# Second layer's shift and scale summed elementwise on VectorE, ScalarE and GpSimd beside the last merges and the output projection of the first

## The chip, the cores and the metric

The kernel runs as one program on one core of a Trainium2 chip. The metric is device time in microseconds (us), from launch to the last store, the median over runs. TensorE (PE in the rows) multiplies matrices, with a row of its own for its weight loads (PEld); VectorE is DVE, ScalarE ACT, GpSimd POOL; SyncE (SP) issues most of the loads. Each engine works through its own instructions strictly in order.

## The reference

Two layers of a backbone with four parallel token mixers (A windowed attention, B RWKV-7, C attention, D gated DeltaNet), model width 2048, 256 context and 256 latent tokens, all fp32. What matters here is the modulation and the tail of a layer:

```
shift, scale, gate = split(silu(c) @ w_mod + b_mod, 3)          # per layer, for latent tokens
sh_c, sc_c, gt_c   = split(silu(c_ctx) @ w_mod + b_mod, 3)      # the same for context tokens
h  = rms(x) * (1 + scale) + shift                               # input of the layer
x  = x + gate * (sum_i sigmoid(pm @ g_up[i] + g_b[i]) * (y_i @ w_br[i])) @ w_out
```

`w_mod` of one layer is 2048 x 6144. There are only two vectors to multiply it with, `c` and `c_ctx`, so the product is 2 x 6144 numbers for 50 MB of weights.

## The kernel before

**Tiles.** Activations stand feature-first: 16 tiles of 128 features by 512 tokens. Most products are made of float32r matmuls with operands split in a high and a low part: `weights` (L370) loads a weight tile of 128x512 into `wr` on SyncE's queue, ScalarE casts it to `wh`, VectorE subtracts to get `wl`, and `mm3` issues three matmuls for each 128x128 block. `wh` and `wl` have 4 buffers each, `wr` has 5.

**The modulation.** `w_mod` is cut in 12 chunks of 512 columns (0 to 3 shift, 4 to 7 scale, 8 to 11 gate), each of 16 tiles of 128 rows by 512 columns, 256 KB. `mod_unit` (L477) handles 4 such tiles: 4 loads on SyncE's queue, then 4 matmuls with 32 columns of `s32` (the two silu vectors, in columns 6 and 7, zeros around them) as weights and the tile as the moving operand, each into its own 32 rows of one PSUM bank. 16 units sum 4 chunks in one bank; after the last a copy to `ms`, four small matmuls with `sel` (which bring the numbers back to feature-first) and additions of the bias give four chunks of `mod`.

**The stage of the change.** In `layer`, the first layer ends with `drain`, which pumps what is left in the queue of generators: the steps of `merge_gen` for the branches C and D (in a step, 18 matmuls give one output tile of gate and branch, with a tanh on ScalarE and a multiply and an add on VectorE). Then `out_proj` makes 16 output tiles `x`, each of 4 weight tiles and 48 matmuls, and behind each of them it calls two units of `next_mods`: 32 units, chunks 0 to 7 of the second layer's modulation, in banks of the pool `mx`. The remaining 16 units (the first layer's generator goes on with the gate chunks 8 to 11 of the second layer) follow in `run`, 8 ahead of `build_h` and 8 among the first projections of layer 1. The loads of all these go to `mr`, which has 16 buffers.

**What sets the order.** The code states work in a sequence, and a scheduler that fills each engine's list by its own planning costs decides the order in which the instructions stand on each engine. That order is fixed when the program is built: an engine whose next instruction waits does not pass over it.

Of the kernel before, what the change touches and what calls it, by code (L numbers as in the profile page):

```python
# [12 lines left out]
AF = mybir.ActivationFunctionType  # L13
ALU = mybir.AluOpType
# [39 lines left out]
_PO, _o = {}, 0  # L54
# [116 lines left out]


MXB = 3
NL2 = 3
MODS = (2, 3)
MODL = (((0, 8, 12),), ())
# [11 lines left out]
class Kern:  # L188
# [8 lines left out]
    def nm(s, t):  # L197
# [2 lines left out]

    BUFS = {t: 2 for t in ("ar AT01 AT10 AT11 tok0 tok1 wc bo vt dl nb dec Dk ktok vs pT pt aq "
                           "iR sw po it").split()}
    BUFS.update(mr=16, Z=3, U=3, S=3, vs=3, dZ=3, Sd=4, Rb=16, po=3, ms=1, wr=5, wh=4, wl=4, QD=3, qg=3, dl=4, vn=2,
                nb=4, dec=4)

    BX = ({}, dict(vtok=2, cz=2))
# [234 lines left out]

    def next_mods(s, pool):

        for n in (0, 4, 8):
            for u in range(16):
                s.mod_unit(s.l + 1 if n < 8 else s.l, tuple(range(n, n + 4)), u, [(pool, "mr")], True, s.bank if n < 8 else None)
                yield

    def mod_gen(s, u):
        s.mod_unit(*u, [(s.wp, "wr")])  # L450
# [26 lines left out]
    def mod_unit(s, l, chunks, u, pools, acc=False, bank=None):  # L477


        nc = s.nc  # L480
        i, nch = u // 4, len(chunks)
        first, last = u == 0, u == 4 * nch - 1
        raws = []
        for g in range(4):
            pool, tag = pools[g % len(pools)]
            raw = s.tl(pool, [128, 512], tag)
            nc.sync.dma_start(raw, s.i["wmod"][l, chunks[i], u % 4 * 4 + g])
            raws.append(raw)
        if first or not acc:
            s.mps = (bank or s.big)()  # L490
        ps = s.mps
        for g in range(4):
            s.mm(ps[32 * g:32 * g + 32, :], s.s32[:, u % 4 * 4 + g, 6 - 2 * i:38 - 2 * i], raws[g],
                 not acc or first, not acc or last)
        if last if acc else first:
            s.ms = s.tl(s.rp, [128, 512], "ms")
            nc.scalar.copy(s.ms, ps)
        elif not acc:
            s.tt(s.ms, s.ms, ps, ALU.add)
        if last:  # L500
            par, mod = s.lp[l]
            bo = _PO["bm"][0]
            w = 2 * nch
            p2 = (bank or s.big)()
            for f in range(4):
                s.mm(p2[:, w * f:w * f + w], s.ms[:, f * 128:(f + 1) * 128], s.c("sel", 0, w))
            pv = p2[:, 0:4 * w].rearrange("p (f i c) -> p i f c", f=4, c=2)
            for i, n in enumerate(chunks):
                s.tt(mod[:, n * 4:n * 4 + 4, :], pv[:, i], wide(par[:, bo + n * 4:bo + n * 4 + 4], 2), ALU.add)


    def sumsq(s, acc, x, first):
# [876 lines left out]
    def out_proj(s, xs_pool):  # L1389
        nc, l, acc = s.nc, s.l, s.acc  # L1390
        t0 = 0 if l == 0 else CTX
        n = T - t0
        ah, al = [], []
        for dt in range(KT):
            hi = s.tl(s.R, [128, T], "Rb", F32R)[:, 0:n]
            lo = s.tl(s.R, [128, T], "Ra", F32R)[:, 0:n]
            s.act(hi, acc[dt], AF.Copy, 0.5)
            s.stt(lo, acc[dt], 0.5, hi.bitcast(F32), ALU.mult, ALU.subtract)
            ah.append(hi)
            al.append(lo)  # L1400
        sqa = s.tl(xs_pool, [128, T], "sqa")[:, 0:n]
        xn = []
        if l == 0:
            s.modn = s.next_mods(xs_pool)
        for dt in range(KT):
            xo = s.tl(s.rp, [128, T], "po")[:, 0:n]
            nc.sync.dma_start(xo, s.i["xT"][dt] if l == 0 else s.x1[dt])
            ps = s.big()[:, 0:n]
            for qt in range(4):
                w = s.weights(s.i["wout"][l, dt, qt], [128, 4, 128])  # L1410
                for k in range(4):
                    kk = qt * 4 + k
                    s.mm3(ps, (w[0][:, k, :], w[1][:, k, :]), (ah[kk], al[kk]), kk == 0, kk == 15)
            x = xs_pool.tile([128, n], F32, tag=f"x{dt}", name=s.nm("x"))
            for hf in range(n // 256):
                sl = slice(hf * 256, hf * 256 + 256)
# [54 lines left out]
    def layer(s):  # L1471
# [8 lines left out]
        with s.tc.tile_pool(name=f"mix{l}", bufs=1) as pool:  # L1480
# [10 lines left out]
        s.rho = 0.0  # L1491

    def run(s):
        tc, nc = s.tc, s.nc
        with ExitStack() as ctx:
# [56 lines left out]
            for l in range(L):  # L1552
# [2 lines left out]
                s.par, s.mod = s.lp[l]  # L1555
                s.layer()
                with tc.tile_pool(name=f"xs{l}", bufs=1) as xp:
                    xn, sqa = s.out_proj(xp)
                    rsb = s.rms_rows(sqa, xp)
                    if l + 1 < L:  # L1560
                        s.l = l + 1
                        s.par, s.mod = s.lp[l + 1]
                        for _ in range(8):
                            next(s.modn)
                        s.build_h(xn, rsb)
# [35 lines left out]
```

## Time and profile before

| | us |
|---|---|
| median of 3 runs (2844.48 to 2854.17) | 2846.87 |
| the profiled execution's own time | 2842.45 |
| its span in the trace | 2840.7 |
| PE busy | 2710.4 (95% of the span) |
| DVE busy | 1856.9 (65%) |
| ACT busy | 1260.0 (44%) |
| POOL busy | 180.0 (6%) |

Busy time is a sum of instruction durations with overlaps counted once. Two neighbouring instructions of VectorE or ScalarE overlap by some 0.08 us in their records, so that the distance from start to start is what one costs in a row of many. A matmul's record is longer than the distance to the next one for the same reason.

### The profile page before, as it was taken

The page shows a single profiled execution, that of the slowest core. Times are in us where ns is not written, and L with a number is a line of the kernel's source. Part 1 is how long each engine was busy: PE and PEld are TensorE (multiplying, and loading weights), DVE is VectorE, ACT ScalarE, POOL GpSimd, SP SyncE. Part 2 cuts the span into 40 slices and gives each one's busy share as a digit, 9 for nine tenths or more (in the row PEclk, how much of TensorE's full clock was granted, in tenths as well). Part 3 has the DMA queues.
Part 4 walks back from the last instruction along what each step waited for, and adds up shares of the span by engine and source line. Part 5 has one row for each costly group of instructions (what it writes and reads, how often), then busy time and mean ns, then how long its engine had stood idle before and what let it go on. Part 6 is the DMA issues. An engine that isn't in the chain of part 4 may idle for free. (4 is left out here: it accounts for less than half of the span.)

```text
span 2840.7 us, 52626 instructions
## 1 busy us (share of the span) xinstructions
PE 2710.4 (95%) x19438; PEld 2056.8 (72%) x19438; DVE 1856.9 (65%) x5255; ACT 1260.0 (44%) x2705; POOL 180.0 (6%) x436
## 2 busy tenths in 40 slices
PE   7998999999999998999999999999999999999897
PEld 3676666677787786777787756776777887867897
DVE  4337776656676777876553354777765687678775
ACT  3334333333354555655442244444443356455553
POOL 0000000000010101000000000010010001100000
PEclk9999999999999999999999999999999999999999
DMA  9753243322342323224537886322332442433465
GB/s 346 261 189 127 83 131 105 127 83 68 115 121 88 100 72 115 79 82 134 170 114 248 279 282 203 96 78 78 93 91 75 157 143 88 133 98 88 144 190 159
DMA packets 210049, 385.80 MB, mean 136 GB/s; under 512 B 24640, under 2 KB 37824, under 8 KB 209792
## 3 DMA queue, kind: packets, MB, share of 16 engines
q1 hardware_dynamic: 199872, 351.23, 39.6%
q0 software_dynamic: 9920, 31.20, 2.9%
q8 instruction: 153, 2.51, 0.4%
q14 instruction: 104, 0.85, 0.1%
HBM read 346.95 MB, written 35.39 MB: 135 GB/s over the span
## 5 line engine op out<-in xcount | busy, mean ns | idle before, releaser
L283 PE MATMUL big<-Rb,wh 128*128 128x512 f32 (+1 forms) x3280 | 1100.7, 364 | 21.3 <-ACT Rb L1325 10.0
L283 PE MATMUL big<-Ra,wh 128*128 128x512 f32 (+1 forms) x2128 | 777.3, 365 | 8.9 <-DVE po L315 5.6
L375 ACT CAST wh<-wr 128x512 fp32r<-128x512 f32 x712 | 438.8, 619 | 762.8 <-PE big L283 576.2
L283 PEld LDWEIGHTS big<-Rb,wh 128*128 128x128 f32 x3280 | 612.1, 191 | 128.8 <-ACT Rb L1325 14.0
L312 DVE TENSOR_TENSOR wl<-wr,wh 128x512 fp32r<-128x512 f32 x712 | 488.4, 688 | 304.3 <-ACT wh L375 280.3
L283 PE MATMUL big<-Ra,wl 128*128 128x512 f32 (+1 forms) x1616 | 597.2, 370 | 6.3 <-DVE wl L312 6.3
L283 PEld LDWEIGHTS big<-Ra,wh 128*128 128x128 f32 x2128 | 407.5, 192 | 84.3 <-issue 9.5
L283 PE MATMUL big<-Rb,wl 128*128 128x512 f32 (+1 forms) x1088 | 380.4, 350 | 1.1 <-DVE wl L312 1.1
L283 PEld LDWEIGHTS big<-Ra,wl 128*128 128x128 f32 x1616 | 310.3, 192 | 53.4 <-DVE wl L312 8.6
L283 PEld LDWEIGHTS big<-Rb,wl 128*128 128x128 f32 x1088 | 207.6, 191 | 26.2 <-DVE wl L312 1.5
L312 DVE TENSOR_TENSOR iX<-iX,it 128x60 f32<-128x60 f32 (+24 forms) x744 | 181.4, 244 | 15.7
L312 DVE TENSOR_TENSOR it<-iB,iX 128x60 f32<-128x60 f32 (+24 forms) x744 | 172.7, 232 | 15.6
L315 DVE SCALAR_TENSOR_TENSOR po<-po,big 128x512 f32<-128x512 f32 (+1 forms) x128 | 70.6, 552 | 77.1 <-PE big L283 74.2
L283 PE MATMUL big<-Rb,wr 128*128 128x256 f32 (+1 forms) x448 | 111.3, 417 | 5.0 <-ACT po L309 3.1
L309 ACT ACTIVATE sw<-S,wc 128x64 f32<-128x64 f32 x96 | 33.4, 348 | 176.2 <-DVE S L315 153.5
L283 PE MATMUL big<-mr,s 128*32 128x512 f32 x384 | 85.2, 617 | 18.3 <-DMA mr<-in_wmod 18.3
L309 ACT ACTIVATE po<-big,gb 128x512 f32<-128x512 f32 (+1 forms) x128 | 74.2, 579 | 57.3 <-PE big L283 41.2
L283 PEld LDWEIGHTS big<-Rb,wr 128*128 128x128 f32 (+1 forms) x448 | 70.6, 179 | 24.1 <-issue 7.3
L283 PE MATMUL sc<-vt,AT 64*64 64x64 f32 x512 | 71.3, 238 | 0.0
L315 DVE SCALAR_TENSOR_TENSOR cz<-raw,par,cz 128x508 f32<-128x508 f32 (+3 forms) x96 | 67.2, 700 | 5.4 <-ACT cz L309 5.0
L632 DVE TENSOR_REDUCE mx<-mx 128x1 f32<-128x512 f32 (+1 forms) x96 | 57.1, 599 | 18.7 <-PE mx L283 17.5
L283 PE MATMUL sc<-vt,tok 64*64 64x64 f32 x448 | 67.5, 232 | 0.0
(371 smaller groups left out, 4033.0 us busy)
## 6 DMA issues: line engine op xcount, KB each, us to landing
wr<-in_win SPq DMA_DIRECT2D x440, 256.0 KB, 2.7
mr<-in_wmod SPq DMA_DIRECT2D x320, 256.0 KB, 5.0
wr<-in_wbr SPq DMA_DIRECT2D x128, 256.0 KB, 2.7
wr<-in_wout SPq DMA_DIRECT2D x128, 256.0 KB, 3.1
wr<-in_wmod SPq DMA_DIRECT2D x64, 256.0 KB, 3.9
wr<-in_gup SPq DMA_DIRECT2D x64, 256.0 KB, 2.6
x<-in_xT SPq DMA_DIRECT2D x16, 256.0 KB, 5.4
po<-y SPq DMA_DIRECT2D x16, 256.0 KB, 3.0
```

The lines of the kernel that those rows point to most:

```text
L283: s.nc.tensor.matmul(o, l, r, start=start, stop=stop)
L309: s.nc.scalar.activation(o, i, f, bias=bias, scale=scale, **k)
L312: s.nc.vector.tensor_tensor(o, a, b, op)
L315: s.nc.vector.scalar_tensor_tensor(o, a, sc, b, op0, op1)
L375: s.nc.scalar.copy(hi, raw)
L632: nc.vector.tensor_reduce(mx[:, hc], ps[:, 0:nk], AX.X, ALU.max)
```

## The change

The second layer's shift and scale (chunks 0 to 7) are no longer made of matmuls over 128 tiles. A tile `mr` is multiplied by the two scalars of its 128 rows, once for `c` and once for `c_ctx`, and summed over the 16 tiles of a chunk: for `c` in `ma0` by one VectorE instruction a tile (multiply by the scalar, add the sum so far); for `c_ctx` by ScalarE into `mt` (two buffers) and an addition into `ma1` on GpSimd. What is left of each chunk is a sum over the 128 partitions, which `total` makes with 8 matmuls for four chunks (weights of 32 columns, one of them ones). The loads of these tiles go to GpSimd's queue, five ahead, in 6 buffers. The work starts with the drain of the first layer, now in `finish`: one tile behind each pump and two behind every third, then 5 behind each output tile. The gate chunks keep their 16 units, in `gate_mods`, with 7 buffers `mg` of their own.

```diff
+MRA, MRO = 5, 5
...
-    BUFS.update(mr=16, Z=3, U=3, S=3, vs=3, dZ=3, Sd=4, Rb=16, po=3, ms=1, wr=5, wh=4, wl=4, QD=3, qg=3, dl=4, vn=2,
+    BUFS.update(mr=6, ma0=5, ma1=5, mg=7, mt=2, Z=3, U=3, S=3, vs=3, dZ=3, Sd=4, Rb=16, po=3, ms=1, wr=5, wh=4, wl=4, QD=3, qg=3, dl=4, vn=2,
...
     def next_mods(s, pool):
-        for n in (0, 4, 8):
-            for u in range(16):
-                s.mod_unit(s.l + 1 if n < 8 else s.l, tuple(range(n, n + 4)), u, [(pool, "mr")], True, s.bank if n < 8 else None)
-                yield
+        l, nc = s.l + 1, s.nc
+        one = s.tl(pool, [128, 39], "mo")
+        nc.vector.memset(one, 0.0)
+        nc.vector.memset(one[:, 7:8], 1.0)
+        todo = [(n, ct) for n in range(8) for ct in range(16)]
+        raws, acc = [], {}
+        def fetch():
+            raws.append(s.tl(pool, [128, 512], "mr"))
+            n, ct = todo[len(raws) - 1]
+            nc.gpsimd.dma_start(raws[-1], s.i["wmod"][l, n, ct])
+        def total(n0):
+            ps = s.bank()
+            for r in range(8):
+                s.mm(ps[32 * (r % 4):32 * (r % 4) + 32, :], one[:, 7 - r:39 - r], acc[n0 + r // 2][r % 2], r < 4, r > 3)
+            s.mod_out(l, tuple(range(n0, n0 + 4)), ps, s.bank)
+        for _ in range(MRA):
+            fetch()
+        for i, (n, ct) in enumerate(todo):
...
+            w = [s.s32[:, ct, 6 + v:7 + v] for v in range(2)]
+            if ct == 0:
+                s.ts(acc[n][0], raws[i], w[0], None, ALU.mult)
+                s.act(acc[n][1], raws[i], AF.Copy, w[1])
+            else:
+                s.stt(acc[n][0], raws[i], w[0], acc[n][0], ALU.mult, ALU.add)
+                t = s.tl(pool, [128, 512], "mt")
+                s.act(t, raws[i], AF.Copy, w[1])
+                nc.gpsimd.tensor_tensor(acc[n][1], acc[n][1], t, ALU.add)
+            if len(raws) < len(todo):
+                fetch()
+            if (n, ct) == (4, 8):
+                total(0)
+            yield
+        total(4)
+    def gate_mods(s, pool):
+        for u in range(16):
+            s.mod_unit(s.l, (8, 9, 10, 11), u, [(pool, "mg")], True)
+            yield
...
-                for _ in range(2):
-                    next(s.modn)
+                for _ in range(MRO):
+                    next(s.modn, None)
...
-        s.drain()
+    def finish(s, pool):
+        s.rho = 0.0
+        s.modn = s.next_mods(pool) if s.l == 0 else iter(())
+        i = 0
+        while s.pump():
+            i += 1
+            for _ in range(1 + (i % 3 == 0)):
+                next(s.modn, None)
...
+        return s.out_proj(pool)
```

How the order of instructions changes is shown at three places. On TensorE, in the output projection of the first layer, the list of before has a group of 8 modulation matmuls between two output tiles (`big` is the PSUM bank of an output tile, `wh` and `wl` the weight halves, `Ra` and `Rb` the split activations):

```order
L283 MATMUL big_16026<-Ra_15809,wh_16083 128x512
L283 MATMUL big_16026<-Rb_15808,wl_16084 128x512
L283 MATMUL mx_15901<-mr_16106,s_4_254 32x512
L283 MATMUL mx_15901<-mr_16108,s_4_254 32x512
L283 MATMUL mx_15901<-mr_16110,s_4_254 32x512
L283 MATMUL mx_15901<-mr_16112,s_4_254 32x512
L283 MATMUL mx_15901<-mr_16118,s_4_254 32x512
L283 MATMUL mx_15901<-mr_16120,s_4_254 32x512
L283 MATMUL mx_15901<-mr_16122,s_4_254 32x512
L283 MATMUL mx_15901<-mr_16124,s_4_254 32x512
L283 MATMUL big_16132<-Rb_15748,wh_16135 128x512
```

In the list of the change the 128 matmuls of this kind are gone from the stage, and 16 of `total` stand there in all: 8 spread over the last merges, 8 behind the fifteenth output tile.

On VectorE, in the merges of branch D, the list of before has this for two steps (`po` is the gate times the branch, `Ra` the running sum of the branches):

```order
L315 SCALAR_TENSOR_TENSOR po_15596<-po_15596,big_15598 128x512
L312 TENSOR_TENSOR wl_15682<-wr_15679,wh_15681 128x512
L312 TENSOR_TENSOR Ra_13381<-Ra_13381,po_15596 128x512
L315 SCALAR_TENSOR_TENSOR po_15632<-po_15632,big_15634 128x512
L312 TENSOR_TENSOR wl_15688<-wr_15685,wh_15687 128x512
L312 TENSOR_TENSOR Ra_13460<-Ra_13460,po_15632 128x512
L312 TENSOR_TENSOR wl_15718<-wr_15715,wh_15717 128x512
```

and the list of the change, for the same two steps, this (`ma` is the sum `ma0` of a chunk):

```order
L316 SCALAR_TENSOR_TENSOR po_15210<-po_15210,big_15212 128x512
L313 TENSOR_TENSOR wl_15320<-wr_15317,wh_15319 128x512
L313 TENSOR_TENSOR Ra_13381<-Ra_13381,po_15210 128x512
L316 SCALAR_TENSOR_TENSOR ma_3608_14945<-mr_15273,s_4_254,ma_3608_14945 128x512
L316 SCALAR_TENSOR_TENSOR ma_3722_15401<-mr_15315,s_4_254,ma_3722_15401 128x512
L316 SCALAR_TENSOR_TENSOR ma_3722_15401<-mr_15357,s_4_254,ma_3722_15401 128x512
L316 SCALAR_TENSOR_TENSOR po_15252<-po_15252,big_15254 128x512
L313 TENSOR_TENSOR wl_15326<-wr_15323,wh_15325 128x512
L313 TENSOR_TENSOR Ra_13460<-Ra_13460,po_15252 128x512
L313 TENSOR_TENSOR wl_15362<-wr_15359,wh_15361 128x512
L316 SCALAR_TENSOR_TENSOR ma_3722_15401<-mr_15393,s_4_254,ma_3722_15401 128x512
L316 SCALAR_TENSOR_TENSOR ma_3722_15401<-mr_15399,s_4_254,ma_3722_15401 128x512
```

The scheduler has drawn the tiles forward: 87 of the 128 stand ahead of the first output tile's addition on VectorE, and all 128 ahead of the fifth's. From the first to the last of them VectorE's list has 120 of these additions, 8 multiplications that start a chunk, 67 `wl`, 32 `po`, 32 `Ra` of the merges, 16 low halves made of `Ra` and `Rb`, 6 `Rb`, 3 sums of squares and 4 pairs of output additions.

On ScalarE the multiplications into `mt` stand between the weight casts in the same way, and on GpSimd the list of the change reads, where before it held nothing between the last store of the mixers and the first projection of layer 1:

```order
L456 DMA mr_14463<-in_wmod 128x512
L477 ISA
L477 TENSOR_TENSOR ma_3480_14460<-ma_3480_14460,mt_14502 128x512
L456 DMA mr_14505<-in_wmod 128x512
L477 TENSOR_TENSOR ma_3480_14460<-ma_3480_14460,mt_14538 128x512
L456 DMA mr_14541<-in_wmod 128x512
L477 TENSOR_TENSOR ma_3480_14460<-ma_3480_14460,mt_14544 128x512
L456 DMA mr_14547<-in_wmod 128x512
```

120 additions and 128 loads stand there, in turn or in short runs of two to five.

## Rows read from the trace of the kernel before

**Rows 1.** Stretches: length, busy (count) of PE, PEld, DVE, ACT, POOL, clock, DMA.

```profile
1331.00:1481.00 150.00, 148.74 (x654) 118.15 (x653) 89.45 (x142) 65.17 (x107) 0.00 (x0) 1.00 0.50 157
1481.00:1675.00 194.00, 194.00 (x955) 140.76 (x957) 64.35 (x111) 48.02 (x78) 0.00 (x0) 1.00 0.78 257
1675.00:1760.00 85.00, 82.90 (x414) 46.55 (x407) 42.91 (x88) 43.25 (x82) 3.80 (x9) 1.00 0.76 257
```

**Rows 2.** Timeline of PE in the output projection: start us, us, engine, instruction.

```profile
1660.15 0.39 PE L283 MATMUL big<-Rb,wh 128*128 128x512 f32 x1
1660.38 0.39 PE L283 MATMUL big<-Ra,wh 128*128 128x512 f32 x1
...
1660.92 1.92 PE L283 MATMUL mx<-mr,s 128*32 128x512 f32 x16
1662.78 0.50 PE L283 MATMUL big<-Rb,wh 128*128 128x512 f32 x1
```

**Rows 3.** Timeline of DVE in the merges of branch D.

```profile
1371.79 0.69 DVE L315 SCALAR_TENSOR_TENSOR po<-po,big 128x512 f32<-128x512 f32 x1 [2.19 <-PE big L283]
1372.39 0.68 DVE L312 TENSOR_TENSOR wl<-wr,wh 128x512 fp32r<-128x512 f32 x1
...
1375.87 0.69 DVE L315 SCALAR_TENSOR_TENSOR po<-po,big 128x512 f32<-128x512 f32 x1 [1.59 <-PE big L283]
```

**Rows 4.** Timeline of DVE: additions of the first two output tiles.

```profile
1481.29 0.88 DVE L315 SCALAR_TENSOR_TENSOR x<-big,mod,po 128x256 f32<-128x256 f32 x2 [0.67 <-issue]
...
1492.11 0.88 DVE L315 SCALAR_TENSOR_TENSOR x<-big,mod,po 128x256 f32<-128x256 f32 x2 [1.55 <-PE big L283]
```

**Rows 5.** Groups of ACT from 1331 to 1525 us: busy, mean ns, idle before and its end.

```profile
L375 ACT CAST wh<-wr 128x512 fp32r<-128x512 f32 x67 | 41.5, 622 | 94.3 <-PE big L283 88.5 <-issue 5.5 <-ACT wh L375 0.3
```

**Rows 6.** Instructions of tiles on POOL, whole span: ns min/median/max.

```profile
L577 POOL CAST ks<-ks x8: 612/961/1072, 781.7 to 1116.9; 64x512 fp32r<-64x512 f32 x8
L701 POOL COPY iX<-cst x24: 397/398/764, 213.5 to 2550.3; 128x256 f32<-128x256 f32 x24
```

**Rows 7.** Timeline of POOL, copies of the mixer's inverse.

```profile
1228.78 0.29 POOL L751 COPY iR<-iE 32x128 f32<-32x128 f32 x1
1229.11 0.66 POOL L752 COPY iR<-iE 32x128 f32<-32x128 f32 x1
1229.82 0.65 POOL L751 COPY iG<-iE 32x128 f32<-32x128 f32 x1
1230.50 0.76 POOL L752 COPY iG<-iE 32x128 f32<-32x128 f32 x1
```

**Rows 8.** Timeline of DVE in the same stretch.

```profile
1228.85 0.77 DVE L312 TENSOR_TENSOR Ra<-Ra,po 128x512 f32<-128x512 f32 x1
1229.54 0.77 DVE L312 TENSOR_TENSOR wl<-wr,wh 128x512 fp32r<-128x512 f32 x1
...
1230.43 0.68 DVE L312 TENSOR_TENSOR wl<-wr,wh 128x512 fp32r<-128x512 f32 x1
```

**Rows 9.** Timeline of POOL and DVE at 782 us, attention's key casts.

```profile
781.71 3.77 POOL L577 CAST ks<-ks 64x512 fp32r<-64x512 f32 x4 [4.57 <-ACT ks L574]
...
781.60 1.71 DVE L312 TENSOR_TENSOR ks<-aq,ks 64x512 fp32r<-64x512 f32 x2 [0.69 <-ACT ks L574]
783.34 0.99 DVE L312 TENSOR_TENSOR wl<-wr,wh 128x512 fp32r<-128x512 f32 x1
```

**Rows 10.** Timeline of POOL: a DMA issue.

```profile
1070.19 0.54 POOL L401 DMA_DIRECT2D p_Cq<-po  x1 [1.29 <-DVE iX L312]
```

**Rows 11.** Timeline of POOL: its last instruction ahead of the stage.

```profile
1329.98 0.54 POOL L464 DMA_DIRECT2D y<-sg  x1 [34.11 <-DMA po<-y]
```

**Rows 12.** DMA issues: KB each, median us to landing.

```profile
mr<-in_wmod SPq DMA_DIRECT2D x320, 256.0 KB, 5.0
...
y<-sg POOLq DMA_DIRECT2D x8, 256.0 KB, 2.9
```

**Rows 13.** Stretch of the mixers in which PE was short of work.

```profile
1050.00:1100.00 50.00, 42.86 (x217) 31.65 (x216) 43.38 (x142) 29.74 (x71) 5.79 (x19) 0.93 0.32 101
```

More of the change, by code (lines that the diff above doesn't have):

```diff
@@ L442, in next_mods @@
     def next_mods(s, pool):
-        for n in (0, 4, 8):
-            for u in range(16):
-                s.mod_unit(s.l + 1 if n < 8 else s.l, tuple(range(n, n + 4)), u, [(pool, "mr")], True, s.bank if n < 8 else None)
-                yield
+        l, nc = s.l + 1, s.nc
[17 more added lines that the diff above has]
+            if ct == 0:
+                acc[n] = [s.tl(pool, [128, 512], "ma%d" % v) for v in range(2)]
+            w = [s.s32[:, ct, 6 + v:7 + v] for v in range(2)]
+            if ct == 0:
+                s.ts(acc[n][0], raws[i], w[0], None, ALU.mult)
[15 more added lines that the diff above has]
+            yield
     def mod_gen(s, u):
@@ L500, in mod_unit, with mod_out @@
         if last:
[L501 to L509, printed above, removed]
+            s.mod_out(l, chunks, None, bank)
+    def mod_out(s, l, chunks, ps=None, bank=None):
+        if ps is not None:
+            s.ms = s.tl(s.rp, [128, 512], "ms")
+            s.nc.scalar.copy(s.ms, ps)
+        par, mod = s.lp[l]
+        bo = _PO["bm"][0]
+        w = 2 * len(chunks)
+        p2 = (bank or s.big)()
+        for f in range(4):
+            s.mm(p2[:, w * f:w * f + w], s.ms[:, f * 128:(f + 1) * 128], s.c("sel", 0, w))
+        pv = p2[:, 0:4 * w].rearrange("p (f i c) -> p i f c", f=4, c=2)
+        for i, n in enumerate(chunks):
+            s.tt(mod[:, n * 4:n * 4 + 4, :], pv[:, i], wide(par[:, bo + n * 4:bo + n * 4 + 4], 2), ALU.add)
     def sumsq(s, acc, x, first):
@@ L1402, in out_proj @@
         xn = []
-        if l == 0:
-            s.modn = s.next_mods(xs_pool)
         for dt in range(KT):
@@ L1487, in layer @@
                 s.sidestep()
-        s.drain()
+    def finish(s, pool):
[6 more added lines that the diff above has]
+                next(s.modn, None)
         for u in s.modq:
             s.mod_unit(*u, [(s.wp, "wr")])
-        s.rho = 0.0
+        return s.out_proj(pool)
     def run(s):
@@ L1557, in run @@
                 with tc.tile_pool(name=f"xs{l}", bufs=1) as xp:
-                    xn, sqa = s.out_proj(xp)
+                    xn, sqa = s.finish(xp)
                     rsb = s.rms_rows(sqa, xp)
                     if l + 1 < L:
+                        for _ in s.modn:
+                            pass
                         s.l = l + 1
                         s.par, s.mod = s.lp[l + 1]
+                        s.modn = s.gate_mods(xp)
                         for _ in range(8):
```

## The prediction

> **What bounds the kernel now.** I read the stretches of the stage first [rows 1]. In the merges and the output projection, 1331 to 1675 us, TensorE is busy 342.7 of 344 us at full clock: whatever is taken off it there comes off the time, as long as nothing else takes its place. VectorE has room (89.5 of 150 us, then 64.4 of 194), ScalarE more, GpSimd does nothing. Then the timelines, for the price of one instruction. A plain 128x512 matmul comes every 0.227 us; a run of 16 records of the modulation (8 matmuls, each recorded twice) takes 1.86 us from its start to the next matmul's [rows 2]. A step of the merges repeats every 4.08 us, and in it VectorE's elementwise instructions of 128x512 start 0.60 us apart where nothing delays them [rows 3]; I use 0.605. The last step of the reading is where VectorE and GpSimd work at once, which this change makes them do for a long time: see below.
>
> **What is taken off.** 128 matmuls in 16 such runs: 16 x 1.86 = 29.8 us of TensorE. The output additions confirm it: the first two output tiles, with no modulation between, are 10.82 us apart [rows 4], where 15 tiles in a row with 30 units would need 15 x 10.82 + 15 x 1.86 = 190 us, and the output projection takes 194 [rows 1]. `total` gives back 16 matmuls of the same shape, two runs: 3.7 us. The small matmuls behind them, the copy to `ms` and the bias additions stay. Net gain on TensorE: **26.1 us**.
>
> **What is added, and its cover.** 128 instructions on VectorE, 128 on ScalarE, 120 additions and 128 load issues on GpSimd. The loads leave SyncE's queue and add no bytes. None of it is on TensorE's path by itself, and if each engine could use its own idle time it would be free. ScalarE: 128 x 0.62 (a cast's mean, [rows 5]) = 79 us, into more than 200 us of idle time: hidden. VectorE: 128 x 0.605 = 77 us; from the first to the last tile its list has 120 new additions and 67 + 32 + 16 + 6 + 3 = 124 old instructions with two operands in SBUF, 244 x 0.605 = 147.6 us, and about 22 us that read PSUM or one operand. That fits into the stretch too.
>
> The question is the pace. All 128 tiles stand ahead of the fifth output tile in VectorE's list, and the lists are fixed. `mt` has two buffers, so ScalarE can be two tiles ahead of GpSimd at most, and the weight casts that stand behind the next multiplication wait with it; TensorE waits for the casts. So GpSimd, or GpSimd and VectorE together, set how fast this whole stretch runs. Its room: the first load can be issued when GpSimd's last store is out (issue at 1330.0, landing 2.9 us later) and lands 5.0 us after its issue [rows 11, 12]: work from about 1338 us. Unhindered, TensorE would end the fifth output tile at 1481.3 + 4 x 10.82 + 1.86 (`total`) = 1526.5 us. It also has four weight tiles ready: ScalarE's casts wait mostly for TensorE to free a `wh` [rows 5], and 4 x 12 matmuls x 0.227 = 10.9 us. So the tiles cost nothing up to (1526.5 + 10.9 - 1338) / 120 = **1.66 us per tile**, and 120 us per microsecond above that.
>
> **GpSimd's addition of two 128x512 operands** does not occur in the trace. Below: a cast of 512 elements with one operand, 0.61 us at its fastest [rows 6]. Above: the copy of 256 takes 0.40, so 256 more elements cost 0.21 us, and a second stream of 512 read one after the other 0.43: 0.61 + 0.43 = 1.04 us. I take 1.04, since the fixed part is paid once and nothing in the rows speaks for two reads at a time; I keep 0.61 for the range. The Trainium skill (GPSIMD Engine Reference, section Performance versus the Vector engine) has 4497 ns for an addition of 2048 fp32 elements; a quarter, an estimate, is 1.12 us, by which the sum further down would be 9 us longer. A load's issue is 0.54 us [rows 10]. Alone, then, GpSimd would need 1.04 + 0.54 = 1.58 us per tile: just hidden.
>
> **Do VectorE and GpSimd hold each other up?** At 1229 us they meet. GpSimd's copies of one form take 0.29 us, but 0.66, 0.65 and 0.76 while VectorE runs instructions with two operands in SBUF, and two of these in turn take 0.77 instead of 0.69 [rows 7, 8]. At 782 us four casts take 3.77 us together instead of 4 x 0.61 = 2.45, and the `wl` beside them 0.99 [rows 9]. From the start of the first VectorE instruction there to the end of the last cast are 785.48 - 781.60 = 3.88 us, and the lone prices of the seven add up to 3 x 0.605 + 4 x 0.612 = 4.26. So they run nearly one after the other, at 0.91 of the sum. By this row the 244 and the 120 take 0.91 x (147.6 + 120 x 1.04) = 248 us, 2.07 us per tile, and end at 1338 + 248 = 1586. TensorE is then late by 1586 - 1526.5 - 10.9 = **48.6 us**. The Trainium skill (SBUF — State Buffer, section SBUF: two separate sides) says more: the pair of ports that both engines use is an exclusive lock, and whoever comes second is blocked for the whole instruction of the other. By that rule nothing overlaps and the sum is 272 us, 24 us more. The measured 0.91 decides, with the rule as a part of the upper end.
>
> In the merges this means a step of about 5.3 us in place of 4.08: the 2.6 new tiles per step (87 in 33) take 2.6 x 1.645 x 0.91 = 3.9 us and the 2.5 old pairs of operands 1.4. Behind the late `wl` and `wh` the matmuls stand, behind the late `po` the PSUM bank of the next product.
>
> **Gate chunks.** Of the 16 buffers of before about 8 held the current two units and 8 the next; `mg` has 7, its loads stand in SyncE's list in the same place. One tile less at hand, 256 KB at 257 GB/s [rows 1]: 1 us; were it nine, 9 us. TensorE is busy 82.9 of the 85 us there, so little more can be lost.
>
> **Sum.** -26.1 + 48.6 + 1 = +23.5 us. The profiled execution's own time becomes 2842.45 + 23.5 = 2866 (its span 2864); the median of the runs stands 4.4 above that execution, so 2846.87 + 23.5 = **2870 us**.
>
> **Rivals.**
> *It is hidden, and faster.* If the addition is no dearer than a one-operand cast, the sum is 0.91 x (147.6 + 73.4) = 201 us, 1.68 per tile; if VectorE and GpSimd do not delay each other at the length of 512 elements, GpSimd alone needs 1.58. Either is at the threshold of 1.66, and what remains is -26.1 + 1 = -25: 2822 us. For it speaks that the engines idle, against it rows 7 to 9. It decides at 1.87 us per tile, where loss and gain are equal.
> *GpSimd's issues are not covered either.* The forecast lets VectorE work while GpSimd issues loads. But a load waits for VectorE's use of an older tile, and the addition behind it waits with it; with half of the 0.54 exposed the pace is 2.07 + 0.27 = 2.34, the end at 1619, the loss 81 us, the time 2847 + 81 - 25 = 2903. The clock may add to that: where TensorE was busy only 42.9 of 50 us, its granted clock was 0.93 [rows 13]; 7% of the some 190 us of matmuls in the stretch is 13 us more, 2916.
> *It comes out even.* At a pace of 1.80 to 1.94 the loss is 17 to 34 us against 25: within 0.3%, 8.5 us, about what a measurement of this kernel can tell from no change.
> That the change does not do what it says is ruled out by the lists: the matmuls are gone from TensorE's.
>
> **How the numbers follow.** The forecast (slower by 9 to 48 us, up to the rule's 272 us) 0.40; the uncovered issues (more) 0.21; even 0.11; hidden 0.28. So faster 0.28, same 0.11, slower 0.61. With a hidden case above 0.2 the range has to reach it: from 2820, the whole 26.1 us gained, to 2910, between the two figures of the second rival. The forecast's own range is 2856 to 2895.
>
> **What would show it.** Right: GpSimd's additions above 1.04 us in the mean, with `wl` and `ma0` lengthened beyond 0.69; ScalarE's `mt` waiting for GpSimd; TensorE's idle time in the merges waiting for `wl`, `wh` and `po`; the fifth output tile ending near 1575 us, tiles 6 to 16 10.8 us apart, with VectorE back to its old pattern. Wrong: merges that still repeat every 4.1 us, and additions of 0.6 to 0.7 us. The prediction falls if the additions overlap with VectorE's work more than the short copies did, since 120 of them carry the sum.

## The result and the profile after

The changed kernel takes 2983.62 us (median of 4 runs, 2979.61 to 2985.16) against 2845.68 (4 runs, 2844.47 to 2854.17) of the kernel before: the ratio is 1.0476, with a 95% interval of 1.0453 to 1.0499. It is slower, as forecast, but by 138 us and not by 23.5, and lies far above the range of 2820 to 2910. The profiled execution took 2982.9 us, its span is 2980.9.

Where the 140 us between the two spans come from is read from five landmarks, the start of one instruction each:

| landmark | before | after | later by |
|---|---|---|---|
| first store of a layer 0 projection (`p_Bw`) | 185.9 | 202.8 | 16.9 |
| GpSimd's last store of the mixers (`y`, [rows 11]) | 1330.0 | 1345.4 | 15.4 |
| first output tile's addition (`x`, [rows 4]) | 1481.3 | 1605.6 | 124.3 |
| last output tile's addition | 1674.4 | 1799.7 | 125.3 |
| first store of a layer 1 projection | 1738.3 | 1866.7 | 128.4 |
| end of the span | 2840.7 | 2980.9 | 140.2 |

So 15 to 17 us are lost in the first 200 us of the program, where of the change only a number of buffers is at work, 109 in the merges, about nothing on balance in the output projection, 3 at the gate, 12 in layer 1. ("The gate" is here the time from the last output addition to the first store of a layer 1 projection, in which the gate chunks are made.) The instructions behind three of them in GpSimd's timeline, and the output additions (ns min/median/max, first and last start):

```profile
202.78 0.68 POOL L402 DMA_DIRECT2D p_Bw<-po  x1 [202.33 <-ACT po L401]
...
1345.38 0.54 POOL L506 DMA_DIRECT2D y<-sg  x1 [34.11 <-DVE sg L316]
...
1866.65 0.56 POOL L402 DMA_DIRECT2D p_Bw<-po  x1 [186.71 <-ACT po L401]
```

```profile
L316 DVE SCALAR_TENSOR_TENSOR x<-big,mod,po x32: 466/476/485, 1605.6 to 1799.7; 128x256 f32<-128x256 f32 x32
```

The stretches (columns as in [rows 1]) show which engine is full now:

```profile
1331.00:1481.00 150.00, 107.32 (x403) 77.23 (x402) 130.34 (x130) 72.01 (x118) 90.49 (x98) 0.86 0.53 167
1481.00:1606.00 125.00, 91.79 (x345) 66.37 (x345) 121.39 (x126) 66.05 (x108) 92.36 (x89) 0.94 0.52 159
1606.00:1801.00 195.00, 175.80 (x754) 139.20 (x753) 123.20 (x153) 68.50 (x109) 58.79 (x64) 0.96 0.49 152
```

TensorE, 99% busy there before, is at 72 to 73%, and VectorE at 87 and 97%. TensorE's waits from 1331 to 1700 us (total, times, longest) are nearly all for VectorE, those of ScalarE for GpSimd, for loads and for TensorE, which frees `wh` late:

```profile
PE big L284 <- DVE po L316: 55.8, 25, 3.8
PE big L284 <- DVE wl L313: 19.2, 8, 3.9
PE big L284 <- DVE Rb L313: 11.9, 4, 7.3
PE big L284 <- DVE Ra L316: 5.3, 3, 3.4
```

```profile
ACT mt L310 <- POOL ma L477: 69.2, 59, 3.8
ACT wh L376 <- PE big L284: 36.5, 22, 4.9
ACT mt L310 <- DMA mr<-in_wmod: 36.2, 25, 6.0
```

What fills VectorE is seen in its groups from 1359 to 1682 us, the stretch with the tiles (busy us, mean ns, idle before):

```profile
L316 DVE SCALAR_TENSOR_TENSOR ma<-mr,s,ma 128x512 f32<-128x512 f32 x120 | 151.3, 1266 | 1.6 <-DMA mr<-in_wmod 0.3
L313 DVE TENSOR_TENSOR wl<-wr,wh 128x512 fp32r<-128x512 f32 x67 | 88.7, 1325 | 3.1 <-ACT wh L376 2.7
L313 DVE TENSOR_TENSOR Ra<-Ra,po 128x512 f32<-128x512 f32 x32 | 40.1, 1254 | 0.0
L316 DVE SCALAR_TENSOR_TENSOR po<-po,big 128x512 f32<-128x512 f32 x32 | 21.7, 678 | 3.5 <-PE big L284 3.5
```

`wl`, 0.68 us in [rows 3], and `Ra` take 1.3 in the mean, while `po`, which reads PSUM, keeps its 0.68. The long ones are a kind of their own: of the 120 `ma`, 63 take 0.73 to 0.75 us and 54 take 1.6 to 2.3, with three between. GpSimd's additions are lengthened too, but less often and by less: 74 take 1.27 to 1.34 us, 46 take 1.41 or more, most of these about 1.62. The answers on `ma` (min/median/max in ns), and the group of the additions with its mean:

```profile
L316 DVE SCALAR_TENSOR_TENSOR ma<-mr,s,ma x120: 733/752/2306, 1360.0 to 1681.2; 128x512 f32<-128x512 f32 x120
L477 POOL TENSOR_TENSOR ma<-ma,mt x120: 1268/1303/4775, 1360.7 to 1678.4; 128x512 f32<-128x512 f32 x120
...
L477 POOL TENSOR_TENSOR ma<-ma,mt 128x512 f32<-128x512 f32 x120 | 173.8, 1449 | 28.2 <-ACT mt L310 24.0
```

The timelines of both engines at 1500 us (VectorE first) show it at a single instruction:

```profile
1500.51 1.78 DVE L313 TENSOR_TENSOR wl<-wr,wh 128x512 fp32r<-128x512 f32 x1
1502.22 0.74 DVE L316 SCALAR_TENSOR_TENSOR ma<-mr,s,ma 128x512 f32<-128x512 f32 x1
1502.88 0.68 DVE L316 SCALAR_TENSOR_TENSOR Ra<-Ra,Rb 128x512 fp32r<-128x512 f32 x1
1503.49 0.67 DVE L316 SCALAR_TENSOR_TENSOR po<-po,big 128x512 f32<-128x512 f32 x1
1504.08 1.60 DVE L313 TENSOR_TENSOR wl<-wr,wh 128x512 fp32r<-128x512 f32 x1
1505.61 0.68 DVE L313 TENSOR_TENSOR Ra<-Ra,po 128x512 f32<-128x512 f32 x1
```

```profile
1500.46 1.29 POOL L477 TENSOR_TENSOR ma<-ma,mt 128x512 f32<-128x512 f32 x1 [0.52 <-ACT mt L310]
1503.26 0.55 POOL L456 DMA_DIRECT2D mr<-in_wmod  x1 [1.51 <-ACT mt L310]
1503.83 1.29 POOL L477 TENSOR_TENSOR ma<-ma,mt 128x512 f32<-128x512 f32 x1
```

An addition runs from 1500.46 to 1501.75 us, and the `wl` that began 0.05 us later ends 0.54 us after that: it has stood still for the addition and then done its work. The next addition runs to 1505.12 us, and the `wl` of 1504.08 ends at 1505.68, 0.56 later. The `po` that begins ahead of this addition at 1503.49 is not touched; of the 32 `po` six begin while an addition runs, and these last 0.67 to 0.69 us too. Over the whole stretch 115 of VectorE's 244 instructions with two operands in SBUF end 0.56 us after the end of an addition, as these two do; the other way round, 44 of the 46 long additions end some 1.15 us after the end of a VectorE instruction of this kind that was running when they began.

### The profile page after: what moved, and what is told of

Same layout as the page of the kernel before. It is cut to its first block, busy times and chain, and to the rows that moved or that the text cites. A ratio compares the mean times of both kernels' runs of the same rounds, so it can differ in the third digit from the quotient of the medians.

```text
span 2980.9 us, 52847 instructions
## 1 busy us (share of the span) xinstructions
PE 2753.7 (92%) x19214; PEld 2080.4 (70%) x19214; DVE 2068.6 (69%) x5385; ACT 1342.1 (45%) x2833; POOL 420.4 (14%) x684
## 4 chain that ended last, share of the span: by engine, by line
PE 33%; DVE 10%; issue 6%; ACT 2%; POOL 2%; DMA 2%; DVEq 0%; SPq 0%; POOLq 0%; ACTq 0%
PE big L284 22%; PE mx L284 6%; PE sc L284 3%; DVE ma L316 2%; DVE wl L313 2%; POOL ma L477 1%; PE mx L306 1%; DVE iX L313 1%; PE acc L284 1%; DVE it L313 1%; DVE Ra L313 1%; DMA mr<-in_wmod 1%; DVE po L316 1%; ACT pt L310 0%; ACT wh L376 0%
## 5 line engine op out<-in xcount | busy, mean ns | idle before, releaser
L284 PE MATMUL big<-Rb,wh 128*128 128x512 f32 (+1 forms) x3280 | 1124.6, 372 | 88.6 <-DVE po L316 56.2
L284 PEld LDWEIGHTS big<-Rb,wh 128*128 128x128 f32 x3280 | 624.1, 196 | 203.6 <-DVE po L316 70.2
L313 DVE TENSOR_TENSOR wl<-wr,wh 128x512 fp32r<-128x512 f32 x712 | 531.2, 748 | 259.8 <-ACT wh L376 239.8
L284 PE MATMUL big<-Rb,wl 128*128 128x512 f32 (+1 forms) x1088 | 393.9, 363 | 20.2 <-DVE wl L313 20.1
L284 PEld LDWEIGHTS big<-Rb,wl 128*128 128x128 f32 x1088 | 215.9, 198 | 51.5 <-DVE wl L313 25.1
L477 POOL TENSOR_TENSOR ma<-ma,mt 128x512 f32<-128x512 f32 x120 | 173.8, 1449 | 28.2 <-ACT mt L310 24.0
L316 DVE SCALAR_TENSOR_TENSOR ma<-mr,s,ma 128x512 f32<-128x512 f32 x120 | 151.3, 1266 | 1.6 <-DMA mr<-in_wmod 0.3
L310 ACT ACTIVATE mt<-mr,s 128x512 f32<-128x512 f32 x120 | 86.3, 721 | 105.8 <-POOL ma L477 69.2
L284 PE MATMUL big<-mr,s 128*32 128x512 f32 x256 | 67.1, 626 | 21.7 <-DMA mr<-in_wmod 21.4
L456 POOL DMA_DIRECT2D mr<-in_wmod x128 | 70.0, 548 | 64.7 <-DVE ma L316 36.2
```

What stands on the lines that cost most here:

```text
L284: s.nc.tensor.matmul(o, l, r, start=start, stop=stop)
L310: s.nc.scalar.activation(o, i, f, bias=bias, scale=scale, **k)
L313: s.nc.vector.tensor_tensor(o, a, b, op)
L316: s.nc.vector.scalar_tensor_tensor(o, a, sc, b, op0, op1)
L456: nc.gpsimd.dma_start(raws[-1], s.i["wmod"][l, n, ct])
L477: nc.gpsimd.tensor_tensor(acc[n][1], acc[n][1], t, ALU.add)
```

## The experiments

The landmarks named are those of the table. A time given without a number of runs is that of one run; the kernel before, run 19 times beside one of the groups, took 2838.21 to 2858.12 us, so a difference of less than some 20 us between single times shows nothing by itself. Each kernel is the changed one with the edit shown, unless it says otherwise.

**The fill's buffers alone.** `mods`, which loads the first layer's modulation while the kernel fills, shares the tag `mr` with `next_mods`; it gets 16 buffers of its own.

```diff
-    BUFS.update(mr=6, ma0=5,
+    BUFS.update(mr=6, mf=16, ma0=5,
...
-                        s.mod_unit(0, (g, 4 + g), u, [(xp, "mr")], True)
+                        s.mod_unit(0, (g, 4 + g), u, [(xp, "mf")], True)
```

> The loads of the modulation tiles in the very first stage (layer 0's shift and scale, before any mixer) get 16 buffers of their own again; the change had cut them to 6 by sharing the name mr. If the 15 us by which the changed kernel is late before the stage of the change begins come from this, the first parked projection is issued at about 186 us again (203 in the changed kernel) and the time falls by 15 to 17 us, to about 2967. If they come from a different order of the first stage, nothing moves.

Measured: 2954.78 us, 29 less. `p_Bw` is back at 185.3, the last store of the mixers comes at 1326.1, the first output tile at 1587.4, 18 us earlier, the last 20 earlier. The first layer's share is as expected; some 9 us more came off in layer 1, which I did not follow and which lies within the spread of single runs.

**Six buffers in the kernel before.**

```diff
-    BUFS.update(mr=16, Z=3,
+    BUFS.update(mr=6, Z=3,
```

> Kernel before, with 6 buffers of mr in place of 16 and nothing else changed. If the fill of the first stage is late in the changed kernel because its loads share the tag mr, the first projection's load is issued near 203 us instead of 186, GpSimd's last store of the mixers near 1345 instead of 1330, and the whole takes 2847 + 15 to 20 = 2862 to 2867, plus whatever the modulation in the output projection then waits for its loads. If the fill is late for another reason, 186 and 2847 stay.

Measured: 2924.34 us.

```profile
201.99 0.67 POOL L401 DMA_DIRECT2D p_Bw<-po  x1 [201.54 <-ACT po L400]
```

The fill is late by the same 16 us (186 before), the first output tile by 16.0. Of the 60 us beyond that most are lost where the kernel before still uses `mr` for 48 units: its output projection takes 228 us in place of 193, the gate 82 in place of 64. The changed kernel has other buffers there, so only the 16 us are its own. Over all the kernels of this document the landmark goes with this number alone: 185 to 189 us in the seven whose fill has 16 buffers, 201 to 203 in the seven with six.

**GpSimd's additions left out** (the second sum is not made):

```diff
-                nc.gpsimd.tensor_tensor(acc[n][1], acc[n][1], t, ALU.add)
```

> GpSimd's 120 additions are left out (the sums of the context's vector then hold one tile each); its 128 loads, ScalarE's multiplications and VectorE's additions stay. Ports (A: VectorE's instructions with two operands in SBUF stand still while GpSimd adds): every ma and wl back to 0.69 to 0.74 us, merge steps back to 4.1 us, the stretch no longer late, about 136 us less: 2847. Load (C: VectorE simply has 128 more instructions than it can carry): stays within 15 us of 2983. Pace of GpSimd (B: its chain of issue, wait and addition holds ScalarE up): as A in time, but wl and ma would stay long.

Measured: 2873.93 us, 110 less than the changed kernel, 27 more than expected (31 between the spans). VectorE's instructions are all short now:

```profile
L316 DVE SCALAR_TENSOR_TENSOR ma<-mr,s,ma x120: 732/749/761, 1360.5 to 1574.5; 128x512 f32<-128x512 f32 x120
```

From the first output tile to the last store of one are 168.1 us (1528.8 to 1696.9) against 194.1 before (1481.3 to 1675.4): the gain of 26 us on TensorE is there. It is outweighed by the fill (16), 32 us in the merges, 3 at the gate and 6 in layer 1. So of the 109 us that the changed kernel loses in the merges 77 go with the additions, and 32 are lost without them. The runs with both sums on VectorE show that only part of these is due to the start of the tiles: there the first output tile comes 45 us later than before (the next run), 19 with the fill repaired, and 13 once VectorE's stop for the first load is gone as well (further down).

**Both sums on VectorE**, 240 multiply-adds there and nothing on GpSimd but the loads:

```diff
-                t = s.tl(pool, [128, 512], "mt")
-                s.act(t, raws[i], AF.Copy, w[1])
-                nc.gpsimd.tensor_tensor(acc[n][1], acc[n][1], t, ALU.add)
+                s.stt(acc[n][1], raws[i], w[1], acc[n][1], ALU.mult, ALU.add)
```

> The context's sums are made by VectorE as well (a second multiply-add per tile), nothing by ScalarE and GpSimd except the loads. Ports (A): VectorE's own work in the stretch is about 182 us of the 322 and 127 are standing still; with 120 more instructions of 0.66 it is 261 and nothing stands still, so the time falls by about 61 us, to 2922, although VectorE does twice the new work. Load (C): 79 us more, 3062.

Measured: 2874.10 us. VectorE has 120 more instructions than in the changed kernel, the same sums are made, and the whole is 110 us faster. It is not the amount of work given to VectorE.

```profile
L316 DVE SCALAR_TENSOR_TENSOR ma<-mr,s,ma x240: 743/750/766, 1361.8 to 1662.7; 128x512 f32<-128x512 f32 x120
```

**VectorE's multiply-adds left out** (the first sum is not made, GpSimd's second is):

```diff
-                s.stt(acc[n][0], raws[i], w[0], acc[n][0], ALU.mult, ALU.add)
```

> VectorE's 120 multiply-adds are left out (the sums of the latent tokens' vector then hold one tile each); ScalarE, GpSimd and the loads stay as they are. Ports (A): 124 old two-operand instructions (75 us) and 120 additions (152 us) share the ports, 227 us, and GpSimd alone needs 120 x 1.82 = 218, against a room of 205: 13 to 22 us late instead of 136, so about 2860 to 2870. Pace of GpSimd (B): its chain still takes 2.7 us per tile, and the time stays within 25 us of 2983. Load (C): as with nothing added, about 2847.

Measured: 2925.02 us, between the two. The additions run from 1361.6 to 1604.8 us, 2.03 us per tile, and VectorE's old instructions are still the ones to pay (groups of VectorE from 1361 to 1606 us):

```profile
L313 DVE TENSOR_TENSOR wl<-wr,wh 128x512 fp32r<-128x512 f32 x62 | 80.9, 1307 | 36.1 <-ACT wh L376 35.6
L313 DVE TENSOR_TENSOR Ra<-Ra,po 128x512 f32<-128x512 f32 x32 | 50.2, 1568 | 0.3
```

So 120 additions beside some 115 old instructions with two operands are already too slow; neither of the theories, as I put them in numbers, had that.

**Five `mt` in place of two**, to loosen ScalarE from GpSimd:

```diff
-    ... mg=7, mt=2, ...
+    ... mg=4, mt=5, ...
```

> Changed kernel with five buffers of mt in place of two (and four of mg in place of seven, which costs at the gate only, up to some 10 us). ScalarE may now be five tiles ahead of GpSimd. Theory of the lockstep (the stretch is slow because ScalarE, with the weight casts behind it, waits for GpSimd's additions to free mt, 69 us of such waits): up to 69 us come back before the first output tile, 1605.6 us becomes some 1540 to 1560. Theory of the ports (VectorE stands still while GpSimd adds, and VectorE's own list of work plus these stops is the length of the stretch): the first output tile moves by less than 10 us, and the waits turn up on another engine.

Measured: 3000.19 us; the first output tile at 1607.0 us (1605.6 in the changed kernel). ScalarE's wait for GpSimd is gone from its list, and others have taken its place:

```profile
ACT mt L310 <- DMA mr<-in_wmod: 78.4, 50, 8.8
ACT wh L376 <- PE big L284: 55.1, 30, 6.7
```

The largest wait of the changed kernel, 69 us, was worth nothing: the theory of the lockstep falls. The end is later by what the gate chunks lose with four buffers in place of seven: 81.3 us from the last output addition to the first store of layer 1, 67.0 in the changed kernel.

**A copy in place of the addition** (one operand on GpSimd; the second sum is not made):

```diff
-                nc.gpsimd.tensor_tensor(acc[n][1], acc[n][1], t, ALU.add)
+                nc.gpsimd.tensor_copy(acc[n][1], t)
```

> Changed kernel, GpSimd copies mt to ma1 in place of adding it (the second sum is left out): one operand instead of two. If any pass of GpSimd through SBUF holds up VectorE, VectorE's instructions with two operands keep two lengths, 0.7 us and the same plus the copy's length, and the first output tile comes between 1530 (additions left out) and 1605 (all there), near 1560 at a copy of some 0.6 us. If only GpSimd instructions with two operands do, VectorE's instructions are all near 0.75 us and the first output tile is near 1530, the time near 2874. If the copies are the ones to wait, as at 1229 us of the kernel before, they are lengthened and VectorE's instructions are not.

Measured: 2909.66 us, the first output tile at 1555.3 (expected near 1560). The groups of VectorE and of GpSimd in the stretch:

```profile
L316 DVE SCALAR_TENSOR_TENSOR ma<-mr,s,ma 128x512 f32<-128x512 f32 x116 | 110.4, 956 | 2.8 <-DMA mr<-in_wmod 1.6
L313 DVE TENSOR_TENSOR wl<-wr,wh 128x512 fp32r<-128x512 f32 x65 | 59.9, 926 | 5.0 <-ACT wh L376 5.0
...
L477 POOL COPY ma<-mt 128x512 f32<-128x512 f32 x120 | 96.8, 807 | 26.1 <-ACT mt L310 24.1
```

Here both pay: the copies last 0.807 us in the mean and 0.626 in the median, and VectorE's instructions stand still for 116 x (0.956 - 0.745) + 65 x (0.926 - 0.687) + 33 x (0.900 - 0.687) = 47 us, 0.39 per copy; the copies are lengthened by 24 us in all (120 x (0.807 - 0.609)). It needs no second operand on GpSimd's side.

**All on VectorE, the fill repaired, and eight steps later**, as a version that may beat both:

```diff
-    BUFS.update(mr=6, ma0=5, ma1=5, mg=7, mt=2, ...
+    BUFS.update(mr=6, mf=16, ma0=5, ma1=5, mg=9, ...
...
         for _ in range(MRA):
             fetch()
+        for _ in range(8):
+            yield
```

> Both sums on VectorE, none on GpSimd, as in the run before of that kind (2874); besides the fill has 16 buffers of its own, mg nine, and the first tile stands eight steps later in the lists. Fill: -17 to -20. First tile: there VectorE stood 8.6 us for the first load, TensorE was busy 20 of 35 us with its clock down to 0.59, some 15 us to get back at most. Theory that both are plain delays ahead of the work: 2836 to 2845, even with or a little faster than the kernel before (2847). Rival: VectorE is the bound from 1362 to 1662 (97% busy) and the late start only shifts its work behind: 2850 to 2855.

Measured: 2837.72 us (median of 10, 2834.63 to 2845.04) against 2847.86 beside it; the ratio is 0.9973, 0.9958 to 0.9988. The fill is repaired, the late start is not: the first tile stands at the same place on VectorE as in the changed kernel, between the same `wl` and `Rb`, whatever the order in which the code states the work. So the time is inside the theory's range, but not by its reason: the stop is there, and the merges are 11 us shorter than in the run before of that kind all the same. The stop in VectorE's timeline, and the stretch:

```profile
1344.80 0.49 DVE L320 TENSOR_SCALAR ma<-mr,s 128x512 f32<-128x512 f32 x1 [8.20 <-DMA mr<-in_wmod]
```

```profile
1330.00:1345.00 15.00, 8.24 (x43) 5.83 (x42) 4.12 (x10) 3.40 (x7) 3.78 (x7) 0.89 0.87 304
1345.00:1360.00 15.00, 13.43 (x45) 10.06 (x46) 12.93 (x21) 5.97 (x10) 3.28 (x6) 0.77 0.60 201
```

**Half on VectorE, half on TensorE.** Chunks 0 to 3 as in the kernel above, chunks 4 to 7 as 16 units of `mod_unit` between the tiles, one tile behind every second pump and four steps behind each output tile; one `total`, at the end:

```diff
-        todo = [(n, ct) for n in range(8) for ct in range(16)]
+        todo = [(n, ct) for n in range(4) for ct in range(16)]
...
             yield
+            if i >= 24 and (i - 24) * 2 % 5 < 2:
+                s.mod_unit(l, (4, 5, 6, 7), (i - 24) * 2 // 5, [(pool, "mr")], True, s.bank)
+                yield
```

> As the other kernel of this pair, but only four of the eight chunks (64 tiles) are summed on VectorE, spread over merges and output projection; the other four stay on TensorE as in the kernel before, as 16 units between the tiles. VectorE gets 128 x 0.75 = 96 us of work into 60 us of room in the merges and 130 in the output projection, so it is no bound any more; TensorE loses 56 matmuls net, 56 x 0.2325 = 13 us. If nothing else is in the way 2847 - 13 + 3 at the gate = 2837, range 2832 to 2845, faster than all others. Rival: any stop of VectorE is passed on to TensorE, since its instructions stand ahead of the casts in a fixed order; then nothing is left of the 13 us and it is 2847 or more.

Measured: 2850.63 us (median of 10), ratio 1.001 (1.000 to 1.002): the rival's number. VectorE stands 7.9 us for the first load here too.

**The first tile really later**, in both kernels: the scalars are read from a copy that depends on the latest gated branch `po` of the merges (its value times zero is added), so that the first tile stands behind four `po` of this stage in VectorE's list in place of one.

```diff
+        sw = s.tl(pool, [128, KT, 2], "sw")
+        s.stt(sw, s.lth[:, 0:32].rearrange("p (k c) -> p k c", c=2), 0.0, s.s32[:, :, 6:8], ALU.mult, ALU.add)
...
-            w = [s.s32[:, ct, 6 + v:7 + v] for v in range(2)]
+            w = [sw[:, ct, v:v + 1] for v in range(2)]
```

> All on VectorE, as in the run of 2838 us. There the eight steps moved nothing: the first tile stands at the same place of VectorE's list as in the changed kernel, VectorE again stood 8.2 us for the first load, and TensorE was idle 8.3 of the 30 us from 1330 to 1360 with its granted clock at 0.89 and 0.77 (some 5 us more). Here the first tile depends on the fourth product of the merges that comes later, so that it stands behind it in the list. Theory of the start-up stop (its 8 us and the clock behind it are lost for good): 2838 - 8 to 12 = 2826 to 2830. Rival (VectorE, 97 to 100% busy from 1360 to 1650, sets the end whatever is ahead): 2836 to 2840.

> Half on VectorE and half on TensorE, as in the run of 2851 us, with the first tile behind the fourth later product as in the other kernel of this pair. There TensorE was idle 7.6 of the 30 us from 1330 to 1360 and its clock at 0.82 and 0.84, 11 us together, about what the 56 matmuls less should have brought. Theory of the start-up stop: 2851 - 8 to 12 = 2839 to 2843. Rival (something else in the merges eats the gain): 2850.

Measured, all on VectorE: **2831.42 us** (median of 4, 2828.59 to 2836.34) against 2846.67 beside it, ratio 0.9952, 0.9937 to 0.9966. By its median it is the fastest of all, 6 us below the one with the stop; the two were run in different groups and their intervals of the ratio overlap, so the total alone does not settle these 6 us, and the time lies 1.4 us above the theory's range. TensorE keeps its work and its clock:

```profile
1330.00:1345.00 15.00, 14.24 (x71) 9.86 (x69) 7.90 (x16) 7.61 (x14) 1.43 (x3) 1.00 0.52 165
1345.00:1360.00 15.00, 14.26 (x61) 11.56 (x62) 11.17 (x19) 7.26 (x12) 3.44 (x7) 1.00 0.97 341
1360.00:1380.00 20.00, 20.00 (x89) 16.25 (x88) 20.00 (x33) 7.23 (x12) 4.38 (x8) 1.00 0.58 186
```

The output additions of the same kernel, and six multiply-adds in a row on VectorE's timeline:

```profile
L316 DVE SCALAR_TENSOR_TENSOR x<-big,mod,po x32: 469/477/487, 1494.2 to 1662.4; 128x256 f32<-128x256 f32 x32
```

```profile
1499.80 4.06 DVE L316 SCALAR_TENSOR_TENSOR ma<-mr,sw,ma 128x512 f32<-128x512 f32 x6
```

The output projection takes 168.2 us from first to last addition, and the first projection of layer 1 is stored at 1728.9 us, 9.5 earlier than before. Half and half: 2845.10 us (median of 10), ratio 0.9997 (0.9985 to 1.001), 5.5 us below its pair and between the numbers of theory and rival. Its last output tile comes 5 us earlier than before (1669.0), but its only `total` runs behind that, at 1677 us, and the first projection of layer 1 is stored at 1738.3, exactly as before; that this is the reason was not tried.

**GpSimd's additions with both repairs**, the fill's buffers and the late first tile:

> The changed kernel with GpSimd's additions, and with both other repairs of the fastest run: 16 buffers of its own for the fill, and the first tile behind the fourth later product. Theory of the ports: the fill's repair brings it to 2955 (measured alone), and the start-up stop of 8 us lies on VectorE, which is the bound here, so another 8 to 12 come off at most: 2943 to 2947; the rest, some 112 to 116 us above the same kernel with both sums on VectorE (2831), is what the additions on GpSimd cost. Rival (the delays at the start make most of the loss, and the additions little): below 2900.

Measured: 2952.84 us, 6 us above the theory's numbers and far from the rival's. The stop is gone here as well (TensorE busy 28.7 of the 30 us from 1330), and from the last store of the mixers to the first output tile it takes 238 us in place of the 261 of the kernel with the fill's repair alone (the store itself comes 5 us later). But 16 of these us are lost again in layer 1, for which I have no cause; the kernel before, run beside it, also took 2856.9 us, 9 more than in the first group. What stands either way: with all else repaired, the last output addition comes at 1761.8 us with GpSimd and at 1662.4 with the same sums on VectorE.

## Why the prediction was wrong

**What held.** TensorE's gain, 26.1 us by the prediction, is 26.0 in the run without GpSimd's additions; part of this match is luck, since a group of modulation matmuls made a tile 2.1 us longer (13.0 against 10.88 us), not 1.86, and one `total` 3.0. Tiles 6 to 15 come 10.88 us apart after the change, as forecast. The mechanism of the loss is the one forecast, "they run nearly one after the other": GpSimd adds, VectorE stands, TensorE waits for `po`, `wl` and `Rb`. The run with twice the work on VectorE and the one with five `mt` rule out VectorE's load and the lockstep; with the lockstep goes the path through ScalarE that the prediction also names ("TensorE waits for the casts"). Even the factor comes out near: the 244 instructions of VectorE by 0.605 (0.66 for the 120 multiply-adds, below) are 155 us, the additions 120 x 1.27 = 152; VectorE stands still for 128 us (the means above 0.745 for `ma` and above 0.687 for the rest: 62.5 for `ma`, 42.7 for `wl`, 18.1 for `Ra`, 4.7 for smaller ones), so the pair takes 283 of 307 us, 0.92 of the sum where the prediction took 0.91 from seven instructions. The Trainium skill (SBUF — State Buffer, section SBUF: two separate sides) has the pair of ports as an exclusive lock that the first to start holds for its whole instruction, against VectorE instructions with two operands in SBUF. The trace agrees that the two exclude each other: a `wl` that begins 0.05 us behind an addition ends 0.54 us after it, and `po`, with one operand in PSUM, keeps 0.68. It does not show that the first always has the ports: of the 115 instructions that end 0.56 us after an addition, 56 begin up to 0.58 us ahead of it by the records. Whether the second can come first, or a record begins before the ports are used, no run here tells.

**The step that failed** is "the 244 and the 120 take 0.91 x (147.6 + 120 x 1.04) = 248 us, 2.07 us per tile, and end at 1338 + 248 = 1586". The last tile is at 1681, and the stretch takes 322 us, 2.68 per tile. Three of its terms (the addition, the multiply-add and the start) were too small, and one was left out. (The trace also has 92 of the 128 tiles ahead of the first output tile's addition on VectorE, where 87 were counted from the list.)

- *The addition*: 1.27 us at its fastest, not 1.04. *The multiply-add* with a scalar of its row is 0.66 from start to start (six in a row take 4.06 us, of which the last record has 0.745), not 0.605. Together 0.91 x (120 x 0.23 + 120 x 0.058) = 31 us. In the Trainium skill (GPSIMD Engine Reference, section Performance versus the Vector engine) a quarter of the 2048-element figure, an estimate, is 1.12 us for the addition, and the trace is above that too.
- *VectorE's other instructions*. The prediction counts "about 22 us that read PSUM or one operand" when it asks whether VectorE has room, and drops them when it works out the pace. But VectorE's list is one queue: what does not share the ports still takes its turn there: 32 x 0.59 for `po`, 8 x 0.4, and four pairs of output additions of 0.88, 26 us.
- *The start*. 1358.7 and not 1338: 15.4 us by the fill, and 5 because the first load is issued 7 us after GpSimd's last store (1352.3), where the prediction gave it 2.9. VectorE then also stands 8.1 us for this load, ahead of the merges' own instructions; with the tiles drawn to the front of its list that was to be seen in the order, and was not looked for. Idle gaps of VectorE later in the stretch are another 9 us (busy 313.3 of 322).

31 + 26 + 9 of the pace and 5 of the start explain 71 of the 80 us by which the tiles end late beyond the fill (1681 - 15.4 - 1586). By the prediction's own formula, 1681 - 15.4 - 1526.5 - 10.9 = 128 us of stall; measured are 109 in the merges and the 27 that the output projection did not gain, 136. In the stretch TensorE's granted clock was 0.86 to 0.96 [rows 1: 1.00], which the forecast's formula has not; I put the 8 us there without a run that shows it.

**What was missed altogether**: `mr` went from 16 buffers to 6, and the fill uses the same tag. 15 to 17 us, shown from both sides (2954.78 with buffers of its own, and `p_Bw` at 202.0 in the kernel before with six).

**The rivals.** "GpSimd's issues are not covered either" names a pace of 2.34 and 2903 to 2916 us, nearest to the truth but by another reason: exposed issues would leave VectorE idle, by 0.27 us for each of 120 tiles, 32 us, and it is idle for 9 us in the whole stretch; in the run where GpSimd only issues loads VectorE's multiply-adds stay at 0.749 us. Its remark on the clock did come true in kind, with 0.86 to 0.96. "Hidden" decided at 1.87 us per tile; even with half the instructions on VectorE the pace was 2.03.

**Open**: 12 us in layer 1 (from the last output addition to the end 1181.2 us, 1166.3 before, of which the gate has 3), and why this varies between these kernels by as much as 16 us. This loss does not need the change's instructions: the kernel before with six `mr` takes 1114.9 us from the first store of a layer 1 projection to the end, the changed kernel 1114.2, the kernel before 1102.4; and all these are single profiled executions. Open is also most of the 32 us that the merges lose without any addition on GpSimd: taking away the stop for the first load brought the first output tile forward by 6 us.

## What to carry to other kernels

GpSimd is no spare VectorE: while it passes through SBUF, VectorE's instructions with two operands in SBUF wait, so an addition moved there cost VectorE 1.07 us of standing still to save 0.66 of work. When a pace is worked out for an engine that two streams share, add everything in its list, also what the shared resource does not touch, and time the operation on its own before its price carries the sum. Before a buffer count is changed, look for every user of its tag; and with this scheduler a step was moved back by a dependency, not by stating it later.

## What the runs showed of the hardware that was not expected

- A 128x512 addition of two SBUF operands on GpSimd takes 1.27 us at its fastest (of 120), a copy of that size 0.61.
- Both engines pay, and the share differed with the length: beside the additions VectorE stood still for 128 us, and the additions were longer than 1.27 us by 21 us in all; beside the copies it was 47 us against 24; and the short copies of [rows 7] took more than twice their time, VectorE's instructions there 0.08 us more.
- TensorE's granted clock fell behind the stop of some 8 us: with both sums on VectorE, TensorE was busy 8.4 of the 15 us from 1345, and the stretch behind that shows a granted clock of 0.59, which is most of the time at 1.2 GHz. VectorE is full and TensorE waits there, so how much of the time lost is the clock's was not shown. In the run without the stop the clock stays at 1.00 over the same stretch. The row with the stop:

```profile
1360.00:1380.00 20.00, 11.42 (x25) 7.86 (x26) 19.33 (x31) 4.43 (x8) 6.55 (x12) 0.59 0.70 217
```
